# RMSNorm and SiLU on one core: the last four blocks stored as two transfers of 64 KB runs, and VectorE's code placed nearer to a 128-instruction edge

## The chip, the cores and the metric

The kernel runs on one core of a Trainium2 chip. The metric is the time of one execution on the device in microseconds (us); for the kernel before, the median of three runs is 316.91 us (316.90 to 316.97). The profile is of one execution, and its span runs from the first to the last instruction.

The engines that matter here are VectorE (DVE in the profile), ScalarE (ACT) and SyncE (SP). TensorE (PE) works only at the start. Data moves between the chip's large memory (HBM) and the on-chip memory (SBUF, 128 partitions) by 16 DMA engines. Two queues feed them: loads are issued from ScalarE's instruction stream, stores from SyncE's.

## The reference

The input x has 8192 rows of 2048 float32 numbers. Each row is divided by the root of its mean square (plus eps), multiplied by gamma, and passed through SiLU:

```python
rms = np.sqrt(np.mean(x ** 2, axis=-1, keepdims=True) + eps)
out = gamma * x / rms
return (out * (1 / (1 + np.exp(-out)))).astype(np.float32)
```

67.1 MB are read and 67.1 MB written; nothing is used twice.

## The kernel before

The 8192 rows are cut into 16 blocks (`nblk`) of 512 rows. A block puts J = 4 rows on each of the 128 partitions, so it is 128 x 8192 numbers, 4.19 MB. The blocks live in a ring `xt` of six places (`BUFS`); block b has place b % 6 and is worked on in place: loaded, multiplied, put through SiLU and stored from the same bytes. `rows(b, j, k)` names k rows of block b from the j-th on; in each partition they lie one behind the other.

Which rows of x a block holds is said by `view` (L37). Normally a partition holds four neighbouring rows of x, one run of 32 KB in HBM. For the pair of blocks 4 and 5 (`PAIRS`) a partition holds eight neighbouring rows, four in each block, so the pair has runs of 64 KB and each block takes half of every run. Blocks 4 and 5 are loaded as one transfer (`load_pair`, L69) and stored as two (`store`, L116), whose partitions step 64 KB in HBM.

A block passes through these steps:

- `squares_scalar` (L73) and `squares_vector` (L84): the sums of squares of its four rows, shared between the two engines. `share(b)` rows are ScalarE's (L78), the others VectorE's (L86); in the last blocks it is two and two (one and three in block 12).
- `root` (L93, ScalarE, with a load of the table for the square root ahead of it) and `invert` (L98, VectorE): 1/rms, one number for each row, in `rstd`.
- `multiply` (L103, VectorE): four instructions, one for each row, x times rstd times gamma (L105).
- `silu` (L108, ScalarE): two activations of 128 x 4096, two rows each (L113), and the `store` behind them on SyncE.

Block 15 (`last`) goes another way, so that the product doesn't wait for the root: VectorE multiplies by gamma alone (L177), and ScalarE's activation takes rstd as its scale, one instruction for each row (L179).

The order on each engine is written out by hand (`tc.manual_schedule`): each engine works through its instructions in the order of the program, and an instruction waits where it needs another engine's or a transfer's result. The loop at L145 treats block b and, interleaved with it, the squares and the root of block b + 1. In the middle branch (L158, blocks 3 to 13) the squares of b + 1 come ahead of the product and SiLU of b. In the last branch (L164, block 14) the product comes first; on ScalarE the squares of block 15 come ahead of the SiLU of block 14. The load of block b + 3 is issued on ScalarE behind the first square of block b + 1, and waits for the store of the block that had its place before.

On SyncE there are gamma's load and then the 16 stores in the order of the blocks. At the start, gamma is spread to all partitions by TensorE (L128) and copied out by VectorE (L130).

Of the kernel before, what the change touches and what calls it, by code (L numbers as in the profile page):

```python
# [1 line left out]

# [4 lines left out]

ACT = mybir.ActivationFunctionType
ALU = mybir.AluOpType


@with_exitstack
def kernel(
    ctx: ExitStack,
    tc: tile.TileContext,
    x: bass.AP,
    gamma: bass.AP,
    eps: bass.AP,
    out: bass.AP,
):  # L20

    nc = tc.nc
    P = nc.NUM_PARTITIONS
    f32 = mybir.dt.float32
    x2 = x.flatten_outer_dims()
    o2 = out.flatten_outer_dims()  # L30
    n, d = x2.shape
    J = 4
    BUFS = 6
    nblk = n // (P * J)
    PAIRS = (4,)

    def view(t, b):  # L37

        for q in PAIRS:
            if b in (q, q + 1):  # L40
                both = t[q * P * J:(q + 2) * P * J, :].rearrange("(p j) d -> p (j d)", p=P, j=2 * J)
                return both[:, (b - q) * J * d:(b - q + 1) * J * d]
        return t[b * P * J:(b + 1) * P * J, :].rearrange("(p j) d -> p (j d)", p=P, j=J)

    singles = ctx.enter_context(tc.tile_pool(name="singles", bufs=1))
    small = ctx.enter_context(tc.tile_pool(name="small", bufs=2))
    psum = ctx.enter_context(tc.tile_pool(name="psum", bufs=1, space=bass.MemoryType.PSUM))

    Q = 4
    w = d // Q  # L50
    g = singles.tile([P, d], f32)
    eps_t = singles.tile([P, 1], f32)
    ones = singles.tile([P, P], f32)
    junk_a = psum.tile([P, d], f32, name="junk_a")
    junk_v = psum.tile([P, d], f32, name="junk_v")
    ring = singles.tile([P, BUFS * J * d], f32, name="xt")
    sss, rmss, rstds = {}, {}, {}

    def rows(b, j, k):
        at = (b % BUFS) * J + j  # L60
        return ring[:, at * d:(at + k) * d]

    def row(b, j):
        return rows(b, j, 1)

    def load(b):
        nc.scalar.dma_start(out=rows(b, 0, J), in_=view(x2, b))  # L67

    def load_pair(b):  # L69
        both = x2[b * P * J:(b + 2) * P * J, :].rearrange("(p j) d -> p (j d)", p=P, j=2 * J)  # L70
        nc.scalar.dma_start(out=rows(b, 0, 2 * J), in_=both)

    def squares_scalar(b, loads=()):  # L73


        sss[b] = small.tile([P, J], f32, name="ss")
        for j in range(share(b)):
            nc.scalar.activation(out=junk_a, in_=row(b, j), func=ACT.Square,  # L78
                                 accum_out=sss[b][:, j:j + 1])
            if j == 0:  # L80
                for s in loads:
                    load(s)

    def squares_vector(b):  # L84
        for j in range(share(b), J):
            nc.vector.tensor_tensor_reduce(  # L86
                out=junk_v, in0=row(b, j), in1=row(b, j), scale=1.0, scalar=0.0,
                op0=ALU.mult, op1=ALU.add, accum_out=sss[b][:, j:j + 1])

    def share(b):  # L90
        return 1 if 4 <= b <= 12 and b % 2 == 0 else 2

    def root(b):  # L93
        rms = small.tile([P, J], f32, name="rms")
        nc.scalar.activation(out=rms, in_=sss.pop(b), func=ACT.Sqrt, scale=1.0 / d, bias=eps_t)  # L95
        rmss[b] = rms

    def invert(b):  # L98
        rstd = small.tile([P, J], f32, name="rstd")
        nc.vector.reciprocal(out=rstd, in_=rmss.pop(b))  # L100
        rstds[b] = rstd

    def multiply(b):  # L103
        for j in range(J):
            nc.vector.scalar_tensor_tensor(out=row(b, j), in0=row(b, j), scalar=rstds[b][:, j:j + 1],  # L105
                                           in1=g, op0=ALU.mult, op1=ALU.mult)

    def silu(b, between=()):  # L108
        for h in range(0, J, 2):
            if h:  # L110
                for s in between:
                    load(s)
            nc.scalar.activation(out=rows(b, h, 2), in_=rows(b, h, 2), func=ACT.Silu)  # L113
        store(b)

    def store(b):  # L116
        nc.sync.dma_start(out=view(o2, b), in_=rows(b, 0, J))

    with tc.manual_schedule():

        load(0)
        nc.vector.memset(ones, 1.0)  # L122
        nc.vector.memset(eps_t, float(eps))
        nc.scalar.activation(out=junk_a[:, 0:1], in_=ones[:, 0:1], func=ACT.Square)  # L124
        nc.sync.dma_start(out=g[0:1, :], in_=bass.AP(tensor=gamma.tensor, offset=gamma.offset, ap=[[d, 1], [1, d]]))
        for c in range(Q):
            cols = slice(c * w, (c + 1) * w)
            nc.tensor.matmul(junk_v[:, cols], ones[0:1, :], g[0:1, cols], start=True, stop=True)  # L128
        load(1)
        nc.vector.tensor_copy(out=g, in_=junk_v)  # L130
        nc.scalar.copy(out=junk_a[:, 0:1], in_=junk_v[:, d - 1:d])  # L131
        for b in range(2, PAIRS[0]):
            load(b)
        for b in PAIRS:
            load_pair(b)

        last = nblk - 1
        SOON = 3  # L140
        squares_scalar(0)
        squares_vector(0)
        root(0)
        invert(0)
        for b in range(last):  # L145
            loads = [b + 3] if BUFS + 2 <= b + 3 < nblk else []
            between = []
            if b + 3 == BUFS:

                load(BUFS)  # L150
                between = [BUFS + 1]
            if b < SOON:
                multiply(b)
                squares_scalar(b + 1, loads)
                silu(b)
                squares_vector(b + 1)
                root(b + 1)
            elif b < last - 1:  # L158
                squares_scalar(b + 1, loads)
                squares_vector(b + 1)  # L160
                root(b + 1)
                multiply(b)
                silu(b, between)
            else:  # L164
                multiply(b)
                squares_scalar(b + 1)
                silu(b)
                squares_vector(b + 1)
                root(b + 1)
            if b + 1 < last:  # L170
                invert(b + 1)


        for j in range(J):
            if j == J // 2:
                invert(last)
            nc.vector.tensor_mul(out=row(last, j), in0=row(last, j), in1=g)  # L177
        for j in range(J):
            nc.scalar.activation(out=row(last, j), in_=row(last, j), func=ACT.Silu,  # L179
                                 scale=rstds[last][:, j:j + 1])  # L180
        store(last)


# [1 line left out]
_INS = ['x', 'gamma', 'eps']  # L185
_OUTS = [((8, 1024, 2048), 'float32')]

_NUMBERS = {'eps': 9.999999747378752e-06}


# [26 lines left out]
```

## Time and profile before

| | |
|---|---|
| median of three runs | 316.91 us (316.90 to 316.97) |
| span of the profiled execution | 315.4 us |
| time of the profiled execution beyond its span | not given by the profile; the median is 1.5 us above the span |
| VectorE busy | 235.2 us, 75% |
| ScalarE busy | 212.5 us, 67% |
| load queue (q10), share of 16 DMA engines' span | 49.6% |
| store queue (q1), share of 16 DMA engines' span | 49.3% |
| mean DMA rate | 426 GB/s |

The page's second part cuts the span into 40 slices of 7.9 us and shows one digit for each, the busy share in tenths. `L105` is line 105 of the code. In the lists in order of time, the first two columns are start and duration in us, both from the span's start; `x4` says that four instructions in a row were put together. "DMA to landing" is the time from the instruction that issues a transfer to the last of its data. A line such as `SPq L212 <- DMA out_dram<-xt: 22.5, 3, 9.6` reads: SyncE, at line 212 (the end of the program), waited for stores, 22.5 us in total, three times, 9.6 us the longest. In the table of stages each engine has its busy time and the number of instructions, and the last three columns are the granted clock of TensorE, the DMA's busy share and its GB/s.

### The profile page before, as it was taken

What the parts mean: (1) busy time and instruction counts of PE and PEld (TensorE: products, weight loads), DVE (VectorE), ACT (ScalarE), POOL (GpSimd) and SP (SyncE); (2) the same over time, 40 slices, a digit from 0 to 9 for tenths busy, and PEclk for the clock granted to TensorE, in tenths of its full rate; (3) what the DMA queues carried; (4) which work ended last, traced back from release to release, by engine and by line L of the source; (5) the groups of instructions that cost most, each with busy time, mean ns of one, the idle gap of its engine ahead of it and who ended that gap; (6) DMA issues with size and microseconds to landing.
All of it is one profiled execution on the core that took longest, in us unless ns stands there. A gap on an engine that the chain in (4) does not pass through costs nothing.

```text
span 315.4 us, 436 instructions
## 1 busy us (share of the span) xinstructions
PE 7.2 (2%) x8; PEld 2.5 (1%) x8; DVE 235.2 (75%) x157; ACT 212.5 (67%) x137; POOL 0.2 (0%) x4
## 2 busy tenths in 40 slices
PE   6300000000000000000000000000000000000000
PEld 2000000000000000000000000000000000000000
DVE  0679697944999999999693996939969399994000
ACT  1269998952289968993919849097591999999000
POOL 0000000000000000000000000000000000000000
DMA  8999999999999999999999999999999999999996
GB/s 333 411 453 411 386 532 399 399 440 424 428 437 424 437 432 432 432 432 440 424 440 424 445 420 457 407 457 407 465 399 465 399 465 399 465 403 461 411 453 270
DMA packets 4468, 134.24 MB, mean 426 GB/s; under 512 B 497, under 2 KB 497, under 8 KB 497
## 3 DMA queue, kind: packets, MB, share of 16 engines
q10 hardware_dynamic: 2160, 67.11, 49.6%
q1 hardware_dynamic: 2306, 67.12, 49.3%
q14 instruction: 2, 0.02, 0.0%
HBM read 67.12 MB, written 67.11 MB: 426 GB/s over the span
## 4 chain that ended last, share of the span: by engine, by line
DMA 55%; ACT 18%; DVE 14%; issue 2%; another core or an unknown queue 2%; ACTq 1%; DVEq 0%
DMA out_dram<-xt 40%; DMA xt<-in_x_dram 15%; ACT xt L113 9%; DVE xt L105 9%; DVE junk_v L86 5%; ACT junk_a L78 3%; ACT L95 2%; ACT xt L179 2%; ACT L113 1%; ACTq L212 1%; ACT rms L95 1%; ACTq L67 0%; ACT L179 0%; DVE rstd L100 0%
## 5 line engine op out<-in xcount | busy, mean ns | idle before, releaser
L105 DVE SCALAR_TENSOR_TENSOR xt<-xt,rstd,g 128x2048 f32<-128x2048 f32 x60 | 137.0, 2346 | 0.1
L113 ACT ACTIVATE xt<-xt 128x4096 f32<-128x4096 f32 x30 | 107.3, 3610 | 7.4 <-DVE xt L105 7.3
L86 DVE CUSTOM_DVE_ANT_0 junk_v<-xt 128x2048 f32<-128x2048 f32 x37 | 85.0, 2296 | 26.6 <-DMA xt<-in_x_dram 25.9
L78 ACT ACTIVATE junk_a<-xt 128x2048 f32<-128x2048 f32 x27 | 50.6, 1873 | 34.5 <-DMA out_dram<-xt 22.7
L95 ACT ACT_TABLE_LOAD x15 | 19.2, 1283 | 20.1 <-DMA out_dram<-xt 10.9
L113 ACT ACT_TABLE_LOAD x14 | 18.0, 1283 | 0.2
L100 DVE RECIPROCAL rstd<-rms 128x4 f32<-128x4 f32 x16 | 2.8, 174 | 15.0 <-ACT rms L95 15.0
L130 DVE COPY g<-junk_v 128x2048 f32<-128x2048 f32 x1 | 2.3, 2291 | 9.3 <-PE junk_v L128 9.3
L177 DVE TENSOR_TENSOR xt<-xt,g 128x2048 f32<-128x2048 f32 x4 | 8.9, 2278 | 0.0
L95 ACT ACTIVATE rms<-ss,eps_t 128x4 f32<-128x4 f32 x16 | 4.8, 297 | 5.5 <-DVE ss L86 5.3
L179 ACT ACTIVATE xt<-xt,rstd 128x2048 f32<-128x2048 f32 x4 | 7.7, 1990 | 0.0
L128 PE MATMUL junk_v<-g,ones 1*128 1x512 f32 x8 | 7.2, 1072 | 3.1 <-DMA g<-in_gamma_dram 3.1
L131 ACT COPY junk_a<-junk_v 128x1 f32<-128x1 f32 x1 | 0.1, 144 | 10.1 <-DVE g L130 10.1
L86 DVE DVE_READ_ACCUMULATOR2_ANT ss<- 128x1 f32 x37 | 5.2, 141 | 0.0
L78 ACT ACTIVATION_READ_ACCUMULATOR junk_a<-xt 128x1 f32 x27 | 5.0, 186 | 0.0
L128 PEld LDWEIGHTS junk_v<-g,ones 1*128 1x128 f32 x8 | 2.5, 325 | 6.2 <-issue 6.2
L124 ACT ACT_TABLE_LOAD x1 | 1.3, 1283 | 1.1 <-PEq L198 1.1
L179 ACT ACT_TABLE_LOAD x1 | 1.3, 1283 | 0.0
L122 DVE MEMSET ones<- 128x128 f32 x1 | 0.2, 165 | 0.8 <-PEq L198 0.8
L124 ACT ACTIVATE junk_a<-ones 128x1 f32<-128x1 f32 x1 | 0.2, 174 | 0.0
L198 POOL MEMSET const-bfloat16-1.0<- 128x1 bf16 x1 | 0.1, 103 | 0.0
L198 POOL MEMSET const-uint8-127<- 128x1 uint8 x1 | 0.1, 103 | 0.0
(3 smaller groups left out, 0.3 us busy)
## 6 DMA issues: line engine op xcount, KB each, us to landing
out_dram<-xt SPq DMA_DIRECT2D x16, 4096.0 KB, 39.1
xt<-in_x_dram ACTq DMA_DIRECT2D x14, 4096.0 KB, 26.6
g<-in_gamma_dram SPq DMA_DIRECT2D x1, 8.0 KB
xt<-in_x_dram ACTq DMA_DIRECT2D x1, 61.8
```

The costliest lines, as they stand in the source:

```text
L78: nc.scalar.activation(out=junk_a, in_=row(b, j), func=ACT.Square, accum_out=sss[b][:, j:j + 1])
L86: nc.vector.tensor_tensor_reduce(out=junk_v, in0=row(b, j), in1=row(b, j), scale=1.0, scalar=0.0, op0=ALU.mult, op1=ALU.add, accum_out=sss ...
L95: nc.scalar.activation(out=rms, in_=sss.pop(b), func=ACT.Sqrt, scale=1.0 / d, bias=eps_t)
L100: nc.vector.reciprocal(out=rstd, in_=rmss.pop(b))
L105: nc.vector.scalar_tensor_tensor(out=row(b, j), in0=row(b, j), scalar=rstds[b][:, j:j + 1], in1=g, op0=ALU.mult, op1=ALU.mult)
L113: nc.scalar.activation(out=rows(b, h, 2), in_=rows(b, h, 2), func=ACT.Silu)
L124: nc.scalar.activation(out=junk_a[:, 0:1], in_=ones[:, 0:1], func=ACT.Square)
L128: nc.tensor.matmul(junk_v[:, cols], ones[0:1, :], g[0:1, cols], start=True, stop=True)
L130: nc.vector.tensor_copy(out=g, in_=junk_v)
L177: nc.vector.tensor_mul(out=row(last, j), in0=row(last, j), in1=g)
L179: nc.scalar.activation(out=row(last, j), in_=row(last, j), func=ACT.Silu, scale=rstds[last][:, j:j + 1])
L212: with _tile.TileContext(nc) as tc:
```

## The change

Five things are changed.

- Blocks 12 and 13, and 14 and 15, become pairs (`TAIL`) with runs of 64 KB in HBM, as 4 and 5 are. They are still loaded one by one, each taking half of every run. They are stored in pairs: `store(12)` and `store(14)` do nothing, and `store(13)` and `store(15)` issue one transfer of 8.39 MB for both blocks. Stores go from 16 to 14.
- The SiLU of blocks 12 and 13 is one activation of 128 x 8192 in place of two of 128 x 4096.
- Block 14 is multiplied by gamma alone, in one instruction of 128 x 8192 that reads gamma four times over, and its SiLU takes rstd as its scale in four instructions (`scaled`), as block 15's does.
- In the branch of block 14 this SiLU comes ahead of the squares of block 15 on ScalarE, in place of behind them.
- VectorE's code is padded with at most eight no-operations ahead of its first memset, so that this begins in slot 72 of a block of 128 instructions (`addr_align`). VectorE has three instructions fewer behind it.

```diff
+    TAIL = (12, 14)
+    SLOTS, AT = 128, 72
 
     def view(t, b):
 
-        for q in PAIRS:
+        for q in PAIRS + TAIL:
             if b in (q, q + 1):
...
     def multiply(b):
+        if b == nblk - 2:
+            whole = rows(b, 0, J).rearrange("p (j d) -> p j d", j=J)
+            nc.vector.tensor_mul(out=whole, in0=whole, in1=g.unsqueeze(1).to_broadcast([P, J, d]))
+            return
         for j in range(J):
             nc.vector.scalar_tensor_tensor(out=row(b, j), in0=row(b, j), scalar=rstds[b][:, j:j + 1],
                                            in1=g, op0=ALU.mult, op1=ALU.mult)
 
+    def scaled(b):
+        for j in range(J):
+            nc.scalar.activation(out=row(b, j), in_=row(b, j), func=ACT.Silu,
+                                 scale=rstds[b][:, j:j + 1])
+
     def silu(b, between=()):
-        for h in range(0, J, 2):
+        k = 2 if b < nblk - 4 else J
+        for h in range(0, J, k):
             if h:
                 for s in between:
                     load(s)
-            nc.scalar.activation(out=rows(b, h, 2), in_=rows(b, h, 2), func=ACT.Silu)
+            nc.scalar.activation(out=rows(b, h, k), in_=rows(b, h, k), func=ACT.Silu)
         store(b)
 
     def store(b):
+        if b in TAIL:
+            return
+        if b - 1 in TAIL:
+            both = o2[(b - 1) * P * J:(b + 1) * P * J, :].rearrange("(p j) d -> p (j d)", p=P, j=2 * J)
+            nc.sync.dma_start(out=both, in_=rows(b - 1, 0, 2 * J))
+            return
         nc.sync.dma_start(out=view(o2, b), in_=rows(b, 0, J))
...
         load(0)
+        nc.vector.addr_align(SLOTS, offset=AT, max_nops=8)
         nc.vector.memset(ones, 1.0)
...
             else:
                 multiply(b)
+                scaled(b)
+                store(b)
                 squares_scalar(b + 1)
-                silu(b)
                 squares_vector(b + 1)
                 root(b + 1)
...
-        for j in range(J):
-            nc.scalar.activation(out=row(last, j), in_=row(last, j), func=ACT.Silu,
-                                 scale=rstds[last][:, j:j + 1])
+        scaled(last)
         store(last)
```

## The prediction

> **What bounds the kernel now.** I read the page's first three parts first, to see whether an engine or the DMA sets the pace.
>
> ```profile
> DVE  0679697944999999999693996939969399994000
> ACT  1269998952289968993919849097591999999000
> DMA  8999999999999999999999999999999999999996
> GB/s 333 411 453 411 386 532 399 399 440 424 428 437 424 437 432 432 432 432 440 424 440 424 445 420 457 407 457 407 465 399 465 399 465 399 465 403 461 411 453 270
> q10 hardware_dynamic: 2160, 67.11, 49.6%
> q1 hardware_dynamic: 2306, 67.12, 49.3%
> ```
>
> The DMA row is 9 in all slices but the first and last, and the two queues (q10 loads, q1 stores) fill 98.9% of the span. No engine does that. So the kernel runs as long as 134 MB take, and only two things can change it: a time in which the DMA engines have nothing to move, or a change in how fast they move it. In the last three slices (23.7 us) only the DMA works. The question is therefore whether the stores still reach their queue before it runs dry. I looked at the end next: the landings of the last four stores (window 240 to 316), SyncE's own waits, the bandwidth by stage, and for comparison the landings of the loads.
>
> ```profile
> L117 SPq DMA_DIRECT2D out_dram<-xt x4: 332/332/333, 255.7 to 291.6; - x4
> DMA to landing us min/median/max: 23.1/24.8/29.9
> SPq L212 <- DMA out_dram<-xt: 22.5, 3, 9.6
> 275.50:285.00 9.50, 0.00 (x0) 0.00 (x0) 9.47 (x9) 9.44 (x6) 0.00 (x0) 1.00 0.99 428
> 285.00:295.00 10.00, 0.00 (x0) 0.00 (x0) 2.12 (x1) 6.53 (x4) 0.00 (x0) 1.00 1.02 442
> ```
>
> ```profile
> L67 ACTq DMA_DIRECT2D xt<-in_x_dram x14: 334/334/456, 0.7 to 243.2; - x14
> DMA to landing us min/median/max: 12.3/26.6/61.8
> ```
>
> Store 15 is issued at 291.55 (where ScalarE's last activation ends) and lands 23.1 later, at 314.65; the span ends 0.8 after that. SyncE's last waits are at most 9.6 apart, so a 4.19 MB block takes about 9.65 us (435 GB/s, within the 428 to 449 of the windows here): stores 14, 13, 12 and 11 land near 305.0, 295.3, 285.6 and 276.0. Check: store 12, issued at 255.69, took the 29.9 of the row, and 255.69 + 29.9 = 285.6. So of store 15's 23.1 us some 13 are waiting behind stores 13 and 14. That waiting is the slack that the change spends. The compute at the end, from the order of time:
>
> ```profile
> 255.23 9.13 DVE L105 SCALAR_TENSOR_TENSOR xt<-xt,rstd,g 128x2048 f32<-128x2048 f32 x4
> 262.52 7.12 ACT L113 ACTIVATE xt<-xt 128x4096 f32<-128x4096 f32 x2
> 264.29 0.17 DVE L100 RECIPROCAL rstd<-rms 128x4 f32<-128x4 f32 x1
> 264.49 9.14 DVE L105 SCALAR_TENSOR_TENSOR xt<-xt,rstd,g 128x2048 f32<-128x2048 f32 x4
> 269.88 1.88 ACT L78 ACTIVATE junk_a<-xt 128x2048 f32<-128x2048 f32 x1 [0.24 <-DMA xt<-in_x_dram]
> 273.82 7.11 ACT L113 ACTIVATE xt<-xt 128x4096 f32<-128x4096 f32 x2
> 278.15 4.49 DVE L177 TENSOR_TENSOR xt<-xt,g 128x2048 f32<-128x2048 f32 x2
> 280.94 1.28 ACT L95 ACT_TABLE_LOAD   x1
> 283.85 7.68 ACT L179 ACTIVATE xt<-xt,rstd 128x2048 f32<-128x2048 f32 x4
> ```
>
> ScalarE has silu 13 (262.52), squares 15 (269.88), silu 14 (273.82), root 15 (280.94), silu 15 (283.85 to 291.53), without an idle stretch longer than 0.3 us. VectorE multiplies block 13 from 255.23 to 264.37 and block 14 from 264.49 to 273.6, each a step ahead.
>
> **The change part by part.**
>
> *Silu 12 and 13 in one piece.* One 128x8192 activation in place of two 128x4096 (3.61 each). Against the pair's 7.12 it saves at most one fixed part: a 128x2048 row is 1.87 and a 128x4096 one 3.61, so the fixed part is 0.13 and the whole about 7.05. But the single piece waits for all four multiplied rows. For block 12 they are done at 245.0 and silu 12 starts at 248.54: nothing lost. For block 13 they are done at 264.37, where before the first half began at 262.52: silu 13 runs 264.40 to 271.4, 1.8 later. Squares 15 no longer stand behind it, as the next parts show.
>
> *Block 14 on VectorE.* One 128x8192 product with gamma in place of four products of 2.35 us (9.14 together). No row shows this size. By L177, one 128x2048 product is 2.28 and two in a row 4.49, so four would be 8.9; if the fixed part (0.14, the 128x1 accumulator read) is paid once, 8.7. I take 8.7, since it is one instruction; 8.9 stays for the range. It runs from 264.49 to 273.2. Being one instruction, it frees nothing before its end.
>
> *Block 14 on ScalarE, ahead of squares 15.* Four activations with scale (7.68 in all, as silu 15 now) in place of 7.11. They wait for the product: ScalarE, free at 271.4, idles 1.8 us to 273.2 and is done at 280.9. Behind them on the queue stand squares 15, which had begun at 269.88: two rows are 4.04 us with their accumulator reads (255.57 to 259.61), so root 15 starts at 284.95 instead of 280.94, 4.0 later. VectorE's squares 15 (273.2 to 278) are hidden beside this. Its first two L177 products wait for ScalarE's squares, since they overwrite what these read: they start at about 282.8 and end at 287.3, and the reciprocal behind them is done at 287.5. ScalarE is then still loading its silu table (root 284.95, table and silu at +2.9 as now: 287.86). So silu 15 is 287.86 to 295.54, with 0.4 us to spare, and SyncE's last issue falls at 295.55 instead of 291.55.
>
> *Stores 12 and 13 as one.* Issued at 271.4 (silu 13) instead of 255.69 and 269.66. SyncE waits, nothing else stands in its queue, and no load waits for these blocks. Store 11 keeps the DMA busy until near 275 to 276, so 12 and 13 still stand behind it: cost 0. The load queue ended at 269.85 as before. If the start were slow here, up to a microsecond, the DMA would be done with this pair by 296 instead of 295.3, still ahead of the last pair's first bytes; the cover is the lateness of the last pair itself.
>
> *Stores 14 and 15 as one.* This is where the cost lies. Before, store 14 went out at 280.94, 14 us ahead of its turn. Now its 4.19 MB wait for block 15. The DMA runs dry at 295.3, and the pair of 8.39 MB, 19.3 us at the same rate, is issued at 295.55. Its start into idle engines is no longer hidden. Its price: load 0, the only whole block sent into idle engines, took 12.3 from issue to landing against 9.65 in a full queue, so 2.65; it is a read at the very start, beside gamma's transfer. From the other side, a start that cost nothing would leave +0.2 (295.55 + 19.3 = 314.85). But even gamma's 8 KB, issued at 0.73, let the matmuls start only at 3.13, 2.4 later, so starting from idle is not free; as the lower end I set half of load 0's price, 1.3. I take 2.1, nearer to load 0 as the same size on all engines, a little less because a store has no read of HBM ahead of it. Landing: 295.55 + 19.3 + 2.1 = 316.95 against 314.65: +2.3. With 1.3 it is +1.5, with 2.65 and the 8.9 us product +3.05.
>
> A page of the Trainium skill bears on that price: "DMA: Bandwidth & Descriptors", section "Anatomy of one DMA — SWDGE (gpsimd) path", gives a fixed 2.0 us for each transfer, most of it the receipt of the last write; by that figure the sum would be an estimated +2.2. It is stated for transfers that GpSimd issues, and these are SyncE's.
>
> *Longer runs and the 64 KB stride.* Whatever a packet of 64 KB saves against two of 32 KB is not visible here: blocks 4 and 5 are already loaded as one transfer of 64 KB runs, and in the slices in which it moves (the 4th to the 9th) the bandwidth row averages 428, as elsewhere, so I take 0. Loads 12 to 15 now step 64 KB from partition to partition; stores 4 and 5 do that already, and while they move (after store 3's landing at 127 to about 166) the row stays at 424 to 440 GB/s: 0. For both I keep 0.2 us either way for the range.
>
> *VectorE's code start.* At most eight no-operations ahead of the memsets, hidden by VectorE's 9.3 us of waiting for the gamma matmuls. The page shows two instruction transfers of 8 KB each in the whole span and no VectorE idle that a fetch explains, so there is nothing visible to gain; a stall of some 2 us would vanish in its waits for loads (25.9 us in eight): 0.
>
> **Sum.** +2.3 us on the span of 315.4. The profile gives a span and no time of its own; the timed runs' 316.91 are 1.5 above it, and I carry that over: 316.91 + 2.3 = 319.2.
>
> **Rivals.**
>
> *Faster: each transfer has a fixed cost that merging saves.* With two transfers fewer in a row at the end, and load 0's 2.65 as the price of each, 5.3 us would go; less the 2.3 lost, 3.0 faster: 313.9. It decides the sign from 1.15 us a transfer on. Against it: SyncE's 9.6 us between landings and 442 to 449 GB/s leave no such pause between queued stores. The skill page named above would, read as a sum of 2.0 per transfer, give an estimated 1.7 us gain; the landings here disagree. Chance 0.04.
>
> *No change: the last pair arrives in time.* The pair would have to be issued by about 293. If the large product ran in half the time, ScalarE would be bound by silu 13's end at 271.4 and the issue would fall at 293.75; with the 1.3 us start it would be ready at 295.05, just ahead of the queue's end, and land at 314.6: 316.9, as now. Against it: the 128x2048 forms on VectorE all take 2.28 to 2.35, so nothing there runs at such a rate. Chance 0.05.
>
> *No change: the start from idle is nearly free.* At 0.3 us the pair lands at 315.15, and the time is 317.4, 0.5 above now. For it: the engines and their queue are warm then, which at load 0 they were not. Against it: load 0's 2.65 and gamma's 2.4 are the only starts from idle that the trace has. Chance 0.05.
>
> *Slower still: the repeated gamma rows slow the product.* It reads gamma four times within one instruction, which no row shows. A third more (2.9 us) delays everything behind it: 316.95 + 2.9 is 5.2 above now, 322.1. For it, that the form is new here; against it, that four separate products read the same gamma at 2.28 each. Chance 0.06.
>
> **How the numbers follow.** The forecast, 319.2, holds 0.80; its own bounds are 318.4 (+1.5) and 320.0 (+3.05). Stretched by the stride's 0.2 and a little into the cases on both sides, the range is 318.0 to 320.3. A measurement of this kernel can tell about 0.2%, 0.63 us. Faster: the first rival and a little of the second, 0.05. Same: the two cases of no change, less that little, 0.09. Slower: the forecast and the last rival, 0.86.
>
> **What would show it.** In the profile after: the product as one row near 8.7 us ending near 273.2; ScalarE idle before block 14's activations about 1.8, named VectorE; the root of block 15 near 285; the last issue near 295.5; landing of the last pair some 21.4 after its issue instead of 23.1 for half the bytes; a dip in the DMA row before the last three slices, with about 2 us lost. Wrong would be: a last issue before 293, a pair that lands in under 20.5, or a faster store rate than 435 GB/s.

## The result, and the profile after

The changed kernel takes 318.40 us (median of 5 runs, 318.27 to 318.92); the kernel before, on the same chip, 316.91 us. The ratio is 1.0049, with a 95% interval of 1.0037 to 1.0060: slower by half a per cent, 1.5 us. The profiled execution took 318.4 us, of which the span is 316.6.

The end of the changed kernel in order of time (start, duration, engine, line, operation):

```profile
254.88 9.13 DVE L111 SCALAR_TENSOR_TENSOR xt<-xt,rstd,g 128x2048 f32<-128x2048 f32 x4
264.02 8.66 DVE L108 TENSOR_TENSOR xt<-xt,g 128x8192 f32<-128x8192 f32 x1
264.05 7.03 ACT L125 ACTIVATE xt<-xt 128x8192 f32<-128x8192 f32 x1 [1.98 <-DVE xt L111]
271.11 24.18 SPq L133 DMA_DIRECT2D out_dram<-xt  x2
272.72 7.68 ACT L116 ACTIVATE xt<-xt,rstd 128x2048 f32<-128x2048 f32 x4 [1.64 <-DVE xt L108]
280.30 1.86 ACT L80 ACTIVATE junk_a<-xt 128x2048 f32<-128x2048 f32 x1
284.34 1.28 ACT L97 ACT_TABLE_LOAD   x1
287.24 7.68 ACT L116 ACTIVATE xt<-xt,rstd 128x2048 f32<-128x2048 f32 x4
```

ScalarE now waits twice for VectorE, 1.98 us ahead of block 13's SiLU and 1.64 ahead of block 14's. The root of block 15 starts at 284.34 instead of 280.94. The two pairs of stores go out at 271.11 and, 24.18 less the instruction's own 0.33 later, at about 294.95. Their landings, from the stores' own view:

```profile
L133 SPq DMA_DIRECT2D out_dram<-xt x2: 332/332/332, 271.1 to 294.9; - x2
DMA to landing us min/median/max: 20.7/22.2/23.8
```

And SyncE's waits at the end (in total, times, the longest), one long one in place of three:

```profile
SPq L230 <- DMA out_dram<-xt: 20.3, 1, 20.3
```

The first pair lands at 271.1 + 23.8 = 294.9, before the last pair has moved a byte; the last pair lands 20.73 after its issue, at 315.68, against 314.61 for store 15 before. A packet is what one DMA engine moves in one go, 32 or 64 KB of the blocks here. The table of stages around 295 (length of the stretch, then the engines; the last two columns are the DMA's busy share and GB/s, a packet being counted where it starts), the kernel before first:

```profile
290.00:294.00 4.00, 0.00 (x0) 0.00 (x0) 0.00 (x0) 1.53 (x1) 0.00 (x0) 1.00 1.12 483
294.25:295.75 1.50, 0.00 (x0) 0.00 (x0) 0.00 (x0) 0.00 (x0) 0.00 (x0) 1.00 0.81 350
```

The same stretches of the changed kernel:

```profile
290.00:294.00 4.00, 0.00 (x0) 0.00 (x0) 1.28 (x1) 4.00 (x3) 0.00 (x0) 1.00 0.61 262
294.25:295.75 1.50, 0.00 (x0) 0.00 (x0) 0.00 (x0) 0.67 (x1) 0.00 (x0) 1.00 0.00 0
```

In those 1.5 us no packet starts. The packet records show fewer than 16 in flight from about 293.6 to 295.9, and none from 294.53 to 295.78; averaged over the 16 engines, that is 1.9 us without work. Before, the DMA never paused there.

### The profile page after: what moved, and what is told of

Its sections match the earlier page's. It is cut to its first block, busy times and chain, and to the rows that moved or that the text cites. A ratio compares the mean times of both kernels' runs of the same rounds, so it can differ in the third digit from the quotient of the medians.

```text
span 316.6 us, 435 instructions
## 1 busy us (share of the span) xinstructions
PE 7.2 (2%) x8; PEld 2.5 (1%) x8; DVE 234.7 (74%) x154; ACT 212.8 (67%) x137; POOL 0.2 (0%) x4
## 4 chain that ended last, share of the span: by engine, by line
DMA 42%; DVE 29%; ACT 15%; issue 3%; another core or an unknown queue 2%; ACTq 1%; DVEq 0%
DMA out_dram<-xt 27%; DVE xt L111 16%; DMA xt<-in_x_dram 15%; DVE junk_v L88 10%; ACT xt L125 5%; ACT xt L116 4%; DVE xt L108 3%; ACT junk_a L80 2%; ACT L97 2%; ACT L125 1%; ACTq L230 1%; ACT rms L97 0%; ACT L116 0%; ACTq L69 0%
## 5 line engine op out<-in xcount | busy, mean ns | idle before, releaser
L111 DVE SCALAR_TENSOR_TENSOR xt<-xt,rstd,g 128x2048 f32<-128x2048 f32 x56 | 127.9, 2345 | 0.1
L125 ACT ACTIVATE xt<-xt 128x4096 f32<-128x4096 f32 (+1 forms) x26 | 100.0, 3874 | 9.4 <-DVE xt L111 9.3
L116 ACT ACTIVATE xt<-xt,rstd 128x2048 f32<-128x2048 f32 x8 | 15.4, 1991 | 1.6 <-DVE xt L108 1.6
L108 DVE TENSOR_TENSOR xt<-xt,g 128x8192 f32<-128x8192 f32 x1 | 8.7, 8658 | 0.0
```

The costliest lines, as they stand in the source:

```text
L108: nc.vector.tensor_mul(out=whole, in0=whole, in1=g.unsqueeze(1).to_broadcast([P, J, d]))
L116: nc.scalar.activation(out=row(b, j), in_=row(b, j), func=ACT.Silu, scale=rstds[b][:, j:j + 1])
L125: nc.scalar.activation(out=rows(b, h, k), in_=rows(b, h, k), func=ACT.Silu)
```

## The experiments

In all of them the reasons are these. Theory B: the loss is lateness alone. Block 14 waits for block 15, ScalarE reaches the end of block 15 about 3.4 us later, and the DMA has nothing left to move when the last pair is issued. Against it stand: the longer chain on ScalarE costs time wherever the stores go out (C), the large transfer or its 64 KB runs cost time in themselves (C, D, E), or the count of transfers does (E, F). Theory A was formed from the first comparison of the traces, and is tested in two runs at the end. The ratios are those on record; they differ from the quotient of the two medians by at most 0.0006.

### Stores 14 and 15 one by one

```diff
-        if b in TAIL:
+        if b == TAIL[0]:
             return
-        if b - 1 in TAIL:
+        if b - 1 == TAIL[0]:
```

> The changed kernel with stores 14 and 15 sent one by one again (store 14 behind its own activations, near 280.4); all else as changed. Theory B (the loss is the DMA running dry because block 14 waits for block 15): no dry spell, store 14 follows the pair of 12 and 13, the last block lands near 314.0, time about 316.3 us. Rival C (the longer chain of ScalarE, or the 64 KB runs themselves, cost the time): 318.4 us, as changed.

Measured 316.96 us (11 runs; before 316.93 beside it), ratio 0.9995 (0.9986 to 1.0004). Blocks 12 and 13 are still one transfer, the chain on ScalarE is as long as in the changed kernel, and the last store is issued as late (295.1):

```profile
L135 SPq DMA_DIRECT2D out_dram<-xt x2: 332/332/332, 280.6 to 295.1; - x2
DMA to landing us min/median/max: 19.3/23.8/24.1
```

But store 14 went out at 280.6, so the queue had work until block 15 was ready. The 1.5 us are gone, though not the 2.1 that had been expected. Theory C falls.

### The product of block 14 in four instructions

```diff
-            whole = rows(b, 0, J).rearrange("p (j d) -> p j d", j=J)
-            nc.vector.tensor_mul(out=whole, in0=whole, in1=g.unsqueeze(1).to_broadcast([P, J, d]))
+            for j in range(J):
+                nc.vector.tensor_mul(out=row(b, j), in0=row(b, j), in1=g)
             return
```

> The changed kernel with the product of block 14 as four instructions in place of one, stores still in pairs. Theory B: ScalarE starts block 14 when it is free, 1.64 us sooner; the last issue falls at 293.3, the dry spell of 1.9 us shrinks to 0.1 to 0.3, time 316.7 to 316.9 us. Rival D (a pair of 8.39 MB pays its own start price wherever it is issued): 318.4 us or little less.

Measured 316.87 us, ratio 0.9997 (0.9988 to 1.0006), as theory B has it. The stores are still pairs. ScalarE's 1.64 us of waiting are gone, the squares of block 15 come 1.9 us sooner, and the last pair is issued at 293.04 instead of 294.95. ScalarE at the end, then the pairs' issues:

```profile
270.81 7.67 ACT L116 ACTIVATE xt<-xt,rstd 128x2048 f32<-128x2048 f32 x4
278.38 1.86 ACT L80 ACTIVATE junk_a<-xt 128x2048 f32<-128x2048 f32 x1
L133 SPq DMA_DIRECT2D out_dram<-xt x2: 332/332/333, 270.9 to 293.0; - x2
```

The packet records show 0.1 us without work there instead of 1.9. So the pair of 8.39 MB has no price of its own that this measurement can tell when it comes in time, and one instruction of 8.66 us in place of four was enough to turn the change from neutral to slower.

### The last pair alone, in the kernel before

```diff
     PAIRS = (4,)
+    TAIL = (14,)
...
-        for q in PAIRS:
+        for q in PAIRS + TAIL:
...
     def store(b):
+        if b in TAIL:
+            return
+        if b - 1 in TAIL:
+            both = o2[(b - 1) * P * J:(b + 1) * P * J, :].rearrange("(p j) d -> p (j d)", p=P, j=2 * J)
+            nc.sync.dma_start(out=both, in_=rows(b - 1, 0, 2 * J))
+            return
```

> The kernel before with blocks 14 and 15 as a pair stored in one transfer of 64 KB runs, and nothing else: products, activations and their order stay. The last issue stays near 291.55, 2.5 us ahead of the end of store 13. Theory B (only lateness costs): 316.9 us, no dry spell. Rival D (a pair of 8.39 MB is slow in itself, or block 14's waiting costs wherever it falls): 318.4 us. Rival E (each transfer in the queue has a fixed cost of a microsecond or more): 315.9 us or less.

Measured 317.00 us (before 316.92), ratio 0.9999 (0.9990 to 1.0008). The pair is issued at 291.85, before store 13 ends (295.07), and nothing is lost or gained:

```profile
L122 SPq DMA_DIRECT2D out_dram<-xt x1: 332/332/332, 291.9 to 291.9; - x1
```

Theories D and E both fall: a transfer fewer in a full queue is worth less than the 0.3 us that this measurement can tell.

### Two more activations ahead of block 15's

```diff
+        for _ in range(2):
+            nc.scalar.activation(out=junk_a, in_=row(last, 0), func=ACT.Silu)
         scaled(last)
         store(last)
```

> The changed kernel with two more activations of one row each (into a scratch tile, nothing reads them) on ScalarE ahead of block 15's, about 3.8 us. Theory B (the time is the last issue plus a fixed 20.7 for the pair's start and its bytes, plus what lies behind): the last issue moves to 298.8, the dry spell grows from 1.9 to 5.7 us, time 322.2 us, one for one. Rival (there is other work on the DMA that takes up lateness): less than 320.5 us.

Measured 322.11 us, ratio 1.0158 (1.0142 to 1.0174). ScalarE is 3.80 us longer, the last pair is issued at 298.90, 3.95 later than in the changed kernel, and the time is 3.7 later. In the order of time, the added work:

```profile
287.36 3.80 ACT L199 ACTIVATE junk_a<-xt 128x2048 f32<-128x2048 f32 x2
```

The stores' issues and landings; the last pair lands the same 20.7 after its issue as in the changed kernel:

```profile
L133 SPq DMA_DIRECT2D out_dram<-xt x2: 332/332/332, 271.2 to 298.9; - x2
DMA to landing us min/median/max: 20.7/22.2/23.8
```

And in the table of stages the DMA at 0.00 through three whole microseconds:

```profile
295.00:298.00 3.00, 0.00 (x0) 0.00 (x0) 0.00 (x0) 3.00 (x3) 0.00 (x0) 1.00 0.00 0
```

Once the queue is dry, lateness is paid nearly one for one.

### Pairs as two transfers, and late in earnest

The next edit was meant to keep the lateness and undo the large transfer:

```diff
-            both = o2[(b - 1) * P * J:(b + 1) * P * J, :].rearrange("(p j) d -> p (j d)", p=P, j=2 * J)
-            nc.sync.dma_start(out=both, in_=rows(b - 1, 0, 2 * J))
+            for c in (b - 1, b):
+                nc.sync.dma_start(out=view(o2, c), in_=rows(c, 0, J))
             return
```

> The changed kernel, each pair still issued only when its second block is done, but as two transfers of 4.19 MB, one behind the other. Theory B (lateness alone, and queued transfers have no cost of their own): 318.4 us as changed, within 0.4. Rival E (each transfer costs a microsecond or more, or 64 KB runs move faster): 319.9 us or more.

Measured 316.82 us, ratio 0.9996 (0.9987 to 1.0005): not the 318.4 of theory B. The profile says why, and the mistake was in the edit. Though both are written behind block 15, SyncE waits for each store's own block only:

```profile
255.13 40.03 SPq L133 DMA_DIRECT2D out_dram<-xt  x4
```

The four issues lie at 255.13, 270.98, 280.30 and 294.83, so block 14 was not late, and no time was lost though the last issue was as late as in the changed kernel. To make block 14 late with SyncE working in order, the two were turned round:

```diff
-            for c in (b - 1, b):
+            for c in (b, b - 1):
```

> The changed kernel with each pair stored as two transfers of 4.19 MB, the second block's first: SyncE works in order, so block 14's store is now issued behind block 15's, near 295.2, and really is late (in the run before, the two transfers went out at 280.3 and 294.8, each when its own block was done, so nothing was late). Theory B (lateness alone; neither the number of transfers nor the length of the runs matters): the dry spell of 1.9 us is back, time 318.4 us within 0.4. Rival E (a transfer of 8.39 MB or its 64 KB runs make the loss): 316.9 us. Rival F (each further transfer costs a microsecond): 319.4 us or more.

Measured 318.24 us, ratio 1.0040 (1.0026 to 1.0053). Same bytes, same number of transfers, same 32 KB runs as with the two in order; what differs is the order and time of the issues. Those of blocks 15 and 14 are now at 294.71 and 295.14, and 1.4 us are lost again. Those of blocks 13 and 12 have moved too, to 270.87 and 271.25; the run with stores 14 and 15 apart had shown that to be free, since its pair of 12 and 13 went out at 271.27. The table of stages from 285 on, blocks in order first, then reversed, and below them the reversed run's issues:

```profile
285.00:295.00 10.00, 0.00 (x0) 0.00 (x0) 6.15 (x4) 9.76 (x7) 0.00 (x0) 1.00 1.00 433
285.00:295.00 10.00, 0.00 (x0) 0.00 (x0) 6.04 (x4) 9.64 (x7) 0.00 (x0) 1.00 0.85 367
L133 SPq DMA_DIRECT2D out_dram<-xt x4: 333/352/452, 270.9 to 295.1; - x4
```

The packet records show 1.7 us without work around 295. Rivals E (316.9) and F (319.4 or more) both fall. This is the cleanest pair of the study: it shows lateness without the large transfer, as the four products show the large transfer without lateness.

### VectorE's code start

The first comparison showed two things that the prediction had not: of the two 8 KB packets of code in the span, one comes at 82.1 us instead of 106.5 (the other stays near 93), and block 14's work starts 0.35 us sooner in the changed kernel (its last products for block 13 at 254.88 instead of 255.23). Theory A tied them together. The padding was taken from the changed kernel (first edit), and put alone into the kernel before (second):

```diff
-        nc.vector.addr_align(SLOTS, offset=AT, max_nops=8)
```

```diff
         load(0)
+        nc.vector.addr_align(128, offset=72, max_nops=8)
         nc.vector.memset(ones, 1.0)
```

> The changed kernel without the padding of VectorE's code. Theory A (where VectorE's code crosses the edge decides when its second 8 KB of code are fetched, and that holds up one DMA engine): the fetch, at 82.1 us in the changed kernel, goes back to near 106 as in the kernel before, every load from then on lands about 0.35 us later, the last issue moves from 294.95 to about 295.3, and the time is 318.4 + 0.35 = 318.75 us. Rival (the padding does nothing, as predicted; the 0.35 come from elsewhere): 318.4 us, last issue at 294.95.

> The kernel before with the padding of VectorE's code alone. Theory A: the one DMA engine that was 0.9 us behind the other fifteen at the end is only 0.25 behind, so the time falls by about 0.65 us to 316.25. Rival (the padding does nothing): 316.9 us.

Without the padding the changed kernel takes 318.52 us (318.38 to 318.81; ratio to before 1.0049, 1.0036 to 1.0062), against 318.40 with it; its last issue is at 295.03, its fetch at 106.2. With the padding alone the kernel before takes 316.82 us (before 316.93), ratio 0.9996 (0.9988 to 1.0005), its fetch at 82.5. So the padding of VectorE's code does move the fetch, by 24 us, which shows whose code it is, and the time by nothing that can be told. Theory A falls with the sizes that it gave.

The packet records show a smaller effect of the kind that theory A had in mind. They name no engine, but a packet can be put behind the one that ended just before it. The code packet takes 0.31 us, and the data packet behind it 1.56 us where the fetch is near 82 and 1.75 where it is near 106, in place of 1.21. That engine is 0.65 to 0.68 us later, or 0.84 to 0.89. So the padding gives one engine back about 0.2 us, less than the 0.3 that this measurement can tell.

The 0.35 us don't come from the padding. With the same code ahead of it, VectorE starts block 14's squares at 250.27 in the changed kernel, at 250.09 in the run with four products and at 250.44 in the run with stores 14 and 15 apart, so executions differ by as much; before it was 250.62, and 250.60 with the padding alone. The gap is there by the landing of store 3 (127.14 before, 126.78 changed, 127.12 with the padding alone), long before any block of the tail is loaded. Where it comes from was not pursued.

## Why the prediction was right

The direction, the mechanism and its place were right, and the time lies in the range, near its lower end; the size was too large, 2.3 us forecast and 1.5 measured.

- **Silu 13 and the product.** Forecast: SiLU 13 at 264.40 for 7.05, ScalarE idle 1.8, the product 8.7 long until 273.2. Measured: 264.05, 7.03, 1.64, 8.66, until 272.68. The product behaves as one instruction with one fixed part (as four instructions, in the run with four products, it takes 8.87); gamma read four times over slows nothing, so the last rival is out.
- **The chain to the last issue.** Forecast 295.55, measured 294.95. Of the 0.6, 0.35 are the earlier start of block 14's work, whose source is open and which no term of the forecast holds, about 0.1 that the product starts 0.08 behind its reciprocal and not 0.2, and about 0.1 that the four activations hand over to the squares after 7.58 and not 7.68. The chain itself was costed rightly. VectorE's last products did slip behind ScalarE's squares (282.32) and did not bind.
- **The first pair.** Cost 0, with cover to spare: the DMA works without a pause until 293.6, and block 12's lateness of 15 us is hidden behind store 11.
- **The price of starting from idle.** This is the term that was mis-sized: 2.1 was taken, with 1.3 as the lower end. Measured: 20.7 from issue to landing, less 19.35 for the bytes (eight packets of 64 KB on each engine, 2.418 each), is 1.35; the same in the run with two more activations. Of this, 0.35 lie between the end of the last packet (315.33) and the landing, and store 15 before has them too (314.28 to 314.61), so the start itself costs about 1.0. Load 0 was the wrong row to lean on. In it the first packets start 1.0 to 2.15 us after the issue, engine by engine, and take up to 2.4 instead of 1.2; the last pair's first packets start 0.83 to 0.97 after its issue on all 16 engines and take 2.45 instead of 2.42. Whether load 0 is dearer as a read, by its queue or as the program's first, no run shows; that a store has no read of HBM ahead of it, as the forecast argued, is not shown as the reason. The fixed 2.0 us of the Trainium skill ("DMA: Bandwidth & Descriptors", section "Anatomy of one DMA — SWDGE (gpsimd) path") is also too long here; these are SyncE's transfers.
- **What closes the sum.** 0.6 and 0.75 less than forecast would make +0.95 of +2.3 for the landing, and 315.68 against 314.61 (the forecast has 314.65, from a rounded row) is +1.07. The span ends 0.94 behind the landing instead of 0.82. The last 0.3 lie in the comparison: in every timed execution on record, of every kernel, the time is 1.73 to 1.84 us above that execution's own span. The profiled execution of the kernel before, with its span of 315.4, so took about 317.2 us, 0.3 above the median. The 1.5 that the forecast carried over is the median of some executions less the span of a longer one. It made the forecast 0.3 smaller and brought it nearer to the measurement, which is luck.
- **Why 1.9 us without work cost 1.5.** The forecast lets all engines run dry at one time, 295.3, the landing of store 13. In the changed kernel they run out one by one between 293.6 and 294.53, start again within 0.14 of each other, and their last packets end within 0.15 (315.18 to 315.33). In the kernel before the last packets end between 312.9 and 314.28. Averaged over the engines, 1.0 us is idle before the last packet's end there, 0.3 to 0.7 in the other runs without a pause of note, and 0.1 in the four with one. So the pause takes in a lag that would otherwise cost time at the end; this is worked out from the packets, and no run tests it by itself.
- **Longer runs, the stride, the code start at 0.** Right: the merged pair alone, the split pairs with the 64 KB stride, and the padding alone all lie within 0.11 us of the kernel before, less than their intervals can tell.
- **The rivals.** A fixed cost per queued transfer is refuted by the pair alone in the kernel before. "The pair arrives in time" did not happen, but the run with four products shows that it was 1.9 us away: with the issue at 293.04 the time is 316.87. "The start from idle is nearly free" was out by 1 us: 0.3 was assumed, 1.35 measured.

No version beat the kernel before beyond its interval. Its DMA engines stand idle, on average, for some 2.1 us at the start and about 1 at the end (the lag above), and nothing tried here touches the first.

## What to carry to other kernels

Where the DMA is the bound, the last transfers have slack only as long as earlier ones are queued ahead of them: add up the landings backwards to find when the queue runs dry, and ask of any merge at the end whether its later half is ready by then. Merging transfers in a full queue is worth nothing that could be told here, but it ties the first block's departure to the second's; and one large instruction in place of four gives its reader nothing until it ends. The first load of the program was a poor guide to the price of a late store (2.65 against 1.35). And a median is to be compared with the span of an execution like it: here the two differed by 0.3 us, a fifth of the effect.

## What was not expected

- A start into idle engines costs a store 1.35 us from issue to landing beyond its bytes, against 2.65 for the first load (12.3 less 9.65).
- VectorE's fetch of 8 KB of code went from 106.5 to 82.1 us by moving the code a few slots. It shows as a single packet, and sets one DMA engine back by 0.65 to 0.89 us, which the engine doesn't make up until the DMA runs dry. Why so small a move shifts it by 24 us was not tried.
- In the profiled executions one DMA engine ends behind the other fifteen: 0.9 us behind the next one in the kernel before, 0.24 in the changed one (at its pause), and 0.14 to 0.43 in the others. Followed packet by packet, it is the engine that carried VectorE's code in nine of the ten traces; in the kernel before, two engines lie too close to be told apart. Why the lag is largest there is not known.
